# Half of the last matrix product's columns by seven products, with sums of blocks of m as the stationary operand

## The chip, the cores and the metric

One core of a Trainium2 chip runs the kernel. The metric is the device time of one execution in microseconds (us); lower is better. The engines that matter are TensorE (PE in the profile, with its weight loads as PEld), VectorE (DVE), ScalarE (ACT), GpSimd (POOL, which here issues transfers) and SyncE (SP, which issues the loads of the weights). SBUF is the on-chip memory, PSUM the accumulators that PE writes.

## The reference

One encoder layer for 512 positions of width 2048. The part that is changed is the last product; m comes from the two branches before it:

```python
m = jax.nn.sigmoid(ga) * ya + jax.nn.sigmoid(gb) * yb
x = x + jnp.einsum('bld,de->ble', m, w_o)      # m: 512 x 2048, w_o: 2048 x 2048
return rmsnorm(x, final_g)                      # over the 2048 columns of a row
```

Here `ya` is the output of a gated convolution through `w_out_a` (W_a), `yb` that of a state-space branch through `w_out_b`. All is float32.

## The kernel before

**Numbers in two parts.** Each float32 operand is split in a rounded part `hi` (ACT, a cast) and a rest `lo = x - hi` (DVE, a subtraction), and a product is the sum of three: hi x hi, hi x lo, lo x hi. An operand of the activations in two parts is called `pair` (128 x 2 x 512).

**Weights.** `WStream` holds the weights' loads in order. `W.get()` gives the two parts of the next block of 128 x 1024 numbers (512 KB); `_loads` issues the load on SP's queue (L527, tile `w_raw`), `_hi` the cast (L545, tile `w_hi`), `_lo` the subtraction (L562, `w_lo`). Parts are made two blocks ahead of their use (`ahead`), loads two blocks ahead of that (`lead`); `hi` and `lo` have four buffers each. `add7` gives a group of four blocks for seven products, and makes the sums of blocks that these need on DVE, in place.

**Seven products.** Most products, W_a's last twelve column blocks among them, already work so: a 2 x 2 arrangement of blocks is multiplied with seven block products instead of eight, with sums and differences of blocks as operands (`seven`, `product`, L931 and L936). There the weights are PE's stationary operand and the activations stream. Sums of the activations' blocks (tile `h_comb`) are made by `combine`, from a memory copy that is loaded in 256 KB pieces (tile `h_sum`).

**Order of the work.** The order is written out by hand: side work is a list `bg` of generators, and `step(n)` advances it by n steps between products. A scheduler then places each instruction in its engine's queue. The engines work through their queues in order.

**m and the output product.** `mix` makes m from W_a's product two column blocks at a time and stores it to memory (`m_d`). `reload_m` loads a 512 KB block of it (L1053, tile `m_r`, in the pool `r4b` of six buffers) and splits it into two `pair`s (`split`, L616 and L48). The first four blocks are reloaded during the last seven products of W_a; the last block is split without a trip to memory. Then `omm` multiplies: m is stationary (128 rows of it), 512 columns of W_o stream (L1102 to L1104). Three groups of 512 columns (`n4`) run with four accumulators, one per tile of 128 rows; the fourth group runs row tile by row tile, its weights kept in SBUF by a second stream `W2`, and the last row tile in two halves of 256 columns. `evac` adds x to the accumulator and sums squares; `add_up` and the lines behind it finish a row tile: root, scaling by row and by the gain `fg`, store.

**Buffers.** The large pool `r4` has 37 buffers of 4 KB per partition (`NR4`) for weights, pairs, sums, x and output. In the stage of W_a 16 hold `pair`s and 16 hold `h_comb`.

Of the kernel before, what the change touches and what calls it, by code (L numbers as in the profile page):

```python
# [461 lines left out]
class WStream:  # L462
# [20 lines left out]
    def add7(self, x11, x21, x22, x12):  # L483
# [29 lines left out]
        self.ops.append((lambda: b12["x"], b12, False, None))  # L513
        self.ops.append((lambda: b22["x"], b22, False, None))

    def _loads(self, upto):
        c, nc = self.c, self.c.nc
        while self.nl < len(self.loads) and self.loads[self.nl][0] <= upto:
            i, src, box = self.loads[self.nl]
            self.nl += 1  # L520
            n = src.shape[1] * src.shape[2] if len(src.shape) == 3 else src.shape[1]
            flat = src.rearrange("p a b -> p (a b)") if len(src.shape) == 3 else src
            raw = box["x"] = c.r4.tile([P, SLOT], F32, tag="r4", name="w_raw")
            first = self.ops[i][3]
# [54 lines left out]
def hybrid_kernel(ctx: ExitStack, tc: tile.TileContext, xT, x, cvec, fg, wu, wu7, wabc,  # L579
# [31 lines left out]
    def pair():  # L611
        t = c.r4.tile([P, 2, L], F32R, tag="r4", name="pair")
        return t
# [2 lines left out]
        act.copy(dst[:, 0], src)  # L616
        tt(dst[:, 1], src, dst[:, 0].bitcast(F32), SUB)

    W, W2 = WStream(c, 2, 2), WStream(c, 0, 0)
    for k in range(KD):  # L620
        W.add(wu[k], first=(lambda: scale_x(0)) if k == 0 else None)
    for h in range(2):
# [25 lines left out]
            W.add(wga[j, 2 + h])  # L648
    for j in range(NP7, KD, 2):
        W.add7(wga[j, 2], wga[j + 1, 2], wga[j + 1, 3], wga[j, 3])  # L650
    for n4 in range(4):
        for h in range(8):
            (W2 if n4 == 3 and h < 6 else W).add(wo[n4, h], resident=n4 == 3 and h < 6)


    cv_t = c.cst.tile([P, 106], F32, name="cvec_t")
# [389 lines left out]
        nc.gpsimd.dma_start(m_d[j // 2][:, j % 2], t)  # L1046
    while bg:
        step()
    mp = []

    def reload_m(i):
        t = wide("m_r")
        nc.gpsimd.dma_start(t, m_d[i])  # L1053
        yield
        for n in range(2):
            p = pair()
            split(p, t[:, n])
            mp.append(p)
            yield

    def mix(o, g, t, j):
        stt(g, g, 1.0, o, ADD, MUL)
        yield
        stt(t, t, 0.25, g, MUL, ADD)
        if j < KD - 2:
            nc.gpsimd.dma_start(m_d[j // 2], t)
        yield

    yb7 = blocks(yap, ty7)
    for j in range(NP7, KD, 2):  # L1070
# [6 lines left out]
    for i in range(4, 7):  # L1077
        bg.append(reload_m(i))
    while bg:
        step()  # L1080
    for n in range(2):
        p = pair()
        split(p, mq[-1][1][:, n])
        mp.append(p)


    fgt = [r4b.tile([P, 1024], F32, tag="r4", name="fg") for _ in range(2)]
    for i in range(2):
        nc.gpsimd.dma_start(fgt[i], fg[:, i * 1024:(i + 1) * 1024].to_broadcast([P, 1024]))
    ot = []  # L1090
    for t in range(4):
        for i in range(2):
            o = c.r4.tile([P, 1024], F32, tag="r4", name="o")
            nc.gpsimd.dma_start(o, x[t * P:(t + 1) * P, i * 1024:(i + 1) * 1024])
            ot.append(o)

    def omm(ps, t, w, kk, first, last, c0=0, c1=L):
        hi, lo = (v.rearrange("p (k n) -> p k n", n=L) for v in w)
        for k2 in range(2):
            a = mp[kk * 2 + k2]  # L1100
            cs = slice(t * P, (t + 1) * P)
            nc.tensor.matmul(ps, a[:, 0, cs], hi[:, k2, c0:c1], start=first and k2 == 0, stop=False)  # L1102
            nc.tensor.matmul(ps, a[:, 0, cs], lo[:, k2, c0:c1], start=False, stop=False)  # L1103
            nc.tensor.matmul(ps, a[:, 1, cs], hi[:, k2, c0:c1], start=False, stop=last and k2 == 1)  # L1104

    st = c.cst.tile([P, 4, 8], F32, name="st")

    def chunk(t, n4, a=0, b=L):
        return ot[t * 2 + n4 // 2][:, (n4 % 2) * L + a:(n4 % 2) * L + b]

    def gain(n4, a=0, b=L):
        return fgt[n4 // 2][:, (n4 % 2) * L + a:(n4 % 2) * L + b]

    def evac(ps, t, n4, i, a=0, b=L):
        o = chunk(t, n4, a, b)
        stt(o, ps, 0.25, o, MUL, ADD)
        sq = tmp()
        act.activation(sq[:, :b - a], o, AF.Square, accum_out=st[:, t, i:i + 1])

    def add_up(t, i, scale, bias):  # L1120

# [3 lines left out]
            tt(v, v, st[:, t, n:n + 1], ADD)  # L1125
        ts(v, v, scale, MUL, bias, ADD)

    for n4 in range(3):
        pss = [psum() for _ in range(4)]
        for kk in range(8):  # L1130
            w = W.get()
            for t in range(4):
                omm(pss[t], t, w, kk, kk == 0, kk == 7)
            if n4 == 1 and kk >= 4 or n4 == 2 and kk % 3 == 1:
                W2.prep()
        for t in range(4):
            evac(pss[t], t, n4, n4)
    wl = []
    for t in range(4):
        parts = [(0, L)] if t < 3 else [(0, L // 2), (L // 2, L)]  # L1140
        for n, (a, b) in enumerate(parts):
            ps = psum()[:, :b - a]
            for kk in range(8):
                if t == 0:
                    wl.append(W2.get() if kk < 6 else W.get())
                omm(ps, t, wl[kk], kk, kk == 0, kk == 7, a, b)
            if n == len(parts) - 1:

                add_up(t, 3 + n, 1.0 / D, EPS)
                for i in range(3):  # L1150
                    tt(chunk(t, i), chunk(t, i), gain(i), MUL)
                if a:
                    tt(chunk(t, 3, 0, a), chunk(t, 3, 0, a), gain(3, 0, a), MUL)
            evac(ps, t, 3, 3 + n, a, b)
        last = st[:, t, 2 + len(parts):3 + len(parts)]
        v, r, s = (st[:, t, i:i + 1] for i in (5, 6, 7))
        stt(v, last, 1.0 / D, v, MUL, ADD)
# [91 lines left out]
```

## Time and profile before

| | |
|---|---|
| runs | 1693.05, 1693.30, 1693.66 us, median 1693.3 |
| profiled execution | 1694.92 us in all, span 1693.1 us |
| PE, DVE, ACT busy | 1675.1, 1286.4, 722.4 us |
| matmuls | 8612 |
| moved by transfers | 233.53 MB, mean 138 GB/s |
| loads of W_o | 32 of 512 KB |

The span is the time from the first to the last instruction in the profile. "Busy" is the sum of an engine's instructions; instructions of one engine can overlap a little, so the starts of two that follow each other give the pace. "L931" is line 931 of the kernel. A row of the timeline has start, duration, engine, line, operation, output and inputs; in brackets stands how long the engine stood idle before and what ended that. The granted clock of PE is 1.00 at full rate.

### The profile page before, as it was taken

To read this page: it belongs to the slowest core of one execution; us is meant where nothing else is said; L and a number is where in the kernel's file an instruction comes from. 1 tells how busy PE (TensorE), PEld (TensorE's weight loads), DVE (VectorE), ACT (ScalarE), POOL (GpSimd) and SP (SyncE) were. 2 spreads that over 40 slices of the span, in tenths; PEclk is the share of its full clock that TensorE was granted. 3 is DMA by queue.
4 is the path that set the end of the run, shared out by engine and by line. 5 is a ranking of instruction groups with operands and counts; after the bars stand their busy time and mean duration, and the time that the engine had idled before them with its cause. 6 is when DMAs were issued, how large, how long until landed. Compare 5 with 4: busy or idle time off the path is not lost.

```text
span 1693.1 us, 22360 instructions
## 1 busy us (share of the span) xinstructions
PE 1675.1 (99%) x8612; PEld 1434.0 (85%) x8612; DVE 1286.4 (76%) x1889; ACT 722.4 (43%) x941; POOL 138.9 (8%) x240
## 2 busy tenths in 40 slices
PE   9999999999999999999999999999999999999997
PEld 7888888888888888888888888888888888878887
DVE  7895483948769777698989899998989699974333
ACT  6433423334316422454545554445545444453321
POOL 0003203040100021000000000000000220020000
PEclk9999999999999999999999999999999999999999
DMA  8324345353531454233333433333343855576212
GB/s 303 112 89 133 102 147 113 136 145 103 171 112 54 153 172 157 90 118 116 100 112 102 136 128 108 112 99 115 121 132 130 300 196 179 185 266 256 75 38 100
DMA packets 68331, 233.53 MB, mean 138 GB/s; under 512 B 9152, under 2 KB 9280, under 8 KB 68224
## 3 DMA queue, kind: packets, MB, share of 16 engines
q1 hardware_dynamic: 49392, 170.94, 30.2%
q0 software_dynamic: 18112, 60.06, 11.2%
q8 instruction: 67, 1.10, 0.3%
q10 hardware_dynamic: 720, 1.10, 0.2%
q14 instruction: 40, 0.33, 0.1%
HBM read 203.10 MB, written 24.77 MB: 135 GB/s over the span
## 4 chain that ended last, share of the span: by engine, by line
PE 92%; DVE 4%; DMA 2%; issue 1%; ACT 0%; DVEq 0%; POOL 0%; SPq 0%; ACTq 0%; POOLq 0%
PE ps L931 25%; PE ps L936 13%; PE ps L702 12%; PE ps L701 12%; PE ps L700 12%; PE ps L1103 3%; PE ps L1104 3%; PE ps L1102 3%; PE ps L778 1%; PE ps L779 1%; PE ps L777 1%; DVE w_lo L562 1%; DMA w_raw<-in_wga_dram 1%; PE ps L339 1%; PE ps L434 1%
## 5 line engine op out<-in xcount | busy, mean ns | idle before, releaser
L545 ACT CAST w_hi<-w_raw 128x1024 fp32r<-128x1024 f32 (+2 forms) x347 | 361.7, 1043 | 592.9 <-PE ps L701 246.2
L562 DVE TENSOR_TENSOR w_lo<-w_raw,w_hi 128x1024 fp32r<-128x1024 f32 (+2 forms) x347 | 418.5, 1210 | 242.6 <-ACT w_hi L545 241.9
L700 PE MATMUL ps<-pair,w_hi 128*128 128x512 f32 x912 | 355.8, 390 | 0.0
L702 PE MATMUL ps<-pair,w_lo 128*128 128x512 f32 x912 | 354.4, 389 | 0.7 <-DVE w_lo L562 0.7
L701 PE MATMUL ps<-pair,w_hi 128*128 128x512 f32 x912 | 354.7, 389 | 0.0
L931 PE MATMUL ps<-h_comb,w_hi 128*128 128x512 f32 x1216 | 305.3, 393 | 4.7 <-ACT half L951 4.2
L931 PEld LDWEIGHTS ps<-h_comb,w_hi 128*128 128x128 f32 x1216 | 218.9, 189 | 44.5 <-ACT half L951 4.6
L931 PE MATMUL ps<-pair,w_hi 128*128 128x512 f32 x912 | 230.1, 394 | 0.0
L702 PEld LDWEIGHTS ps<-pair,w_lo 128*128 128x128 f32 x912 | 171.2, 188 | 36.4 <-DVE w_lo L562 1.1
L700 PEld LDWEIGHTS ps<-pair,w_hi 128*128 128x128 f32 x912 | 171.3, 188 | 35.1
L701 PEld LDWEIGHTS ps<-pair,w_hi 128*128 128x128 f32 x912 | 171.3, 188 | 35.1
L931 PEld LDWEIGHTS ps<-pair,w_hi 128*128 128x128 f32 x912 | 165.3, 190 | 29.9
L936 PEld LDWEIGHTS ps<-h_comb,w_lo 128*128 128x128 f32 x1216 | 165.9, 190 | 11.9
L936 PE MATMUL ps<-h_comb,w_lo 128*128 128x256 f32 x1216 | 169.6, 282 | 0.0
L545 ACT CAST w_hi<-w_sum 128x1024 fp32r<-128x1024 f32 x76 | 79.9, 1051 | 139.4 <-DVE w_sum L501 61.5
L936 PEld LDWEIGHTS ps<-pair,w_lo 128*128 128x128 f32 x912 | 125.2, 191 | 9.0
L936 PE MATMUL ps<-pair,w_lo 128*128 128x256 f32 x912 | 127.8, 283 | 0.0
L562 DVE TENSOR_TENSOR w_lo<-w_sum,w_hi 128x1024 fp32r<-128x1024 f32 x76 | 92.6, 1218 | 7.2 <-ACT w_hi L545 7.2
L48 DVE TENSOR_TENSOR half<-ps,half 128x512 f32<-128x512 f32 x114 | 78.0, 684 | 7.2 <-PE ps L936 7.2
L1102 PE MATMUL ps<-w_hi,pair 128*128 128x512 f32 (+1 forms) x212 | 81.6, 385 | 0.0
L1103 PE MATMUL ps<-w_lo,pair 128*128 128x512 f32 (+1 forms) x212 | 81.6, 385 | 0.0
L1104 PE MATMUL ps<-w_hi,pair 128*128 128x512 f32 (+1 forms) x212 | 81.6, 385 | 0.0
(197 smaller groups left out, 1784.5 us busy)
## 6 DMA issues: line engine op xcount, KB each, us to landing
w_raw<-in_wabc_dram SPq DMA_DIRECT2D x128, 512.0 KB, 4.2
w_raw<-in_wga_dram SPq DMA_DIRECT2D x64, 512.0 KB, 4.3
w_raw<-in_wgb_dram SPq DMA_DIRECT2D x48, 512.0 KB, 4.2
w_raw<-in_wo_dram SPq DMA_DIRECT2D x32, 512.0 KB, 7.3
w_raw<-in_wgz_dram SPq DMA_DIRECT2D x24, 512.0 KB, 3.6
w_raw<-in_wu_dram SPq DMA_DIRECT2D x15, 448.0 KB, 7.5
xt<-in_xT_dram SPq DMA_DIRECT2D x16, 256.0 KB, 6.5
ga<-tmp POOLq DMA_DIRECT2D x16, 256.0 KB, 2.4
```

The lines of the kernel that those rows point to most:

```text
L48: return v.tensor_tensor(out=o, in0=a, in1=b, op=op)
L339: nc.tensor.matmul(ps[:, i * NCH:(i + 1) * NCH], self.sl[ri][:, q].rearrange("p g s -> p (g s)"), self.u4[:, q, :], start=True, stop=True)
L545: nc.scalar.copy(hi[:, a:b], raw[:, a:b])
L562: nc.vector.tensor_tensor(out=lo[:, a:b], in0=raw[:, a:b], in1=hi.bitcast(F32)[:, a:b], op=SUB)
L700: nc.tensor.matmul(ps, hi[:, k], a[:, 0], start=first and k == 0, stop=False)
L701: nc.tensor.matmul(ps, hi[:, k], a[:, 1], start=False, stop=False)
L702: nc.tensor.matmul(ps, lo[:, k], a[:, 0], start=False, stop=last and k == 7)
L931: nc.tensor.matmul(ps if flat else both, hi[:, k], a, start=first and k == 0, stop=False, skip_group_check=True)
L936: nc.tensor.matmul(ps[:, HL:], lo[:, k], a[:, :HL] if flat else a[:, 0], start=False, stop=last and k == 7, skip_group_check=True)
L1102: nc.tensor.matmul(ps, a[:, 0, cs], hi[:, k2, c0:c1], start=first and k2 == 0, stop=False)
L1103: nc.tensor.matmul(ps, a[:, 0, cs], lo[:, k2, c0:c1], start=False, stop=False)
L1104: nc.tensor.matmul(ps, a[:, 1, cs], hi[:, k2, c0:c1], start=False, stop=last and k2 == 1)
```

## The change

- Columns 0 to 1023 of the output (`n4` 0 and 1) are computed as before, but with the blocks of the sum in the order `KORD` = 0, 4, 1, 5, 2, 6, 3, 7.
- Columns 1024 to 2047 are computed by seven products. The 2 x 2 blocks of m are its two halves of 256 rows by its two halves of 1024 columns; those of W_o are 1024 x 512 blocks. m's blocks or sums of them (`tm`, tile `m_sum`) stay stationary, 128 rows at a time; W_o's blocks or sums of them stream. One product is 4 weight blocks x 2 row tiles x 6 matmuls.
- `add7_wide` loads the weights for it: 4, 8, 4, 4, 8, 4 and 4 loads for the seven products, since the blocks are loaded again where a sum needs them; 16 sums on DVE.
- m is loaded by `load_y` in two 256 KB pieces and split by `split_m` two steps after the load; the first two steps' buffers come from `r4` (`raw4`). `split_m(0, 2)` runs during the last seven products of W_a (1.7 steps per product instead of 2.7), `split_m(2, 8)` and `sum_m` (which loads all of m again) during the first two column groups, five steps per weight block. The last block of m goes through memory like the others. `fetch_m` is called after `seven` instead of ahead of it.
- `W2` and its resident weights are gone. Accumulators of one product are carried on into the next: `evac` reads them between products. The output rows 256 to 511 are finished after the sixth product, rows 0 to 127 within the seventh, and rows 128 to 255 at the end, in two halves of 256 columns.

The core of the diff:

```diff
-    for n4 in range(4):
-        for h in range(8):
-            (W2 if n4 == 3 and h < 6 else W).add(wo[n4, h], resident=n4 == 3 and h < 6)
+    for n4 in range(2):
+        for h in KORD:
+            W.add(wo[n4, h])
+    W.add7_wide(*([wo[n, 4 * h + i] for i in range(4)] for n in (2, 3) for h in range(2)))
+    def add7_wide(self, x11, x12, x21, x22):
...
+        for x in x11:
+            op(None, keep, (0, x))
+        for s, a, b in zip(sums, x21, x22):
+            op(s, set_(1, 2, ADD), (s, a), (0, b))
+        for s, a in zip(sums, x11):
+            op(s, set_(0, 1, SUB), (0, a))
+        for s, a in zip(sums, x12):
+            op(s, set_(1, 0, SUB), (0, a))
+        for a, b in zip(x11, x21):
+            op(None, set_(1, 2, SUB), (0, a), (0, b))
+        for xs in (x12, x22):
+            for x in xs:
+                op(None, keep, (0, x))
-    def reload_m(i):
-        t = wide("m_r")
-        nc.gpsimd.dma_start(t, m_d[i])
-        yield
-        for n in range(2):
-            p = pair()
-            split(p, t[:, n])
-            mp.append(p)
-            yield
+    def load_y(k, y):
+        for i in range(2):
+            nc.gpsimd.dma_start(y[:, i], m_d[k // 2 + 4 * i][:, k % 2])
+        return y
+    def split_m(a, b, buf):
+        q = []
+        for k in range(a, b + 2):
+            if k < b:
+                q.append(load_y(k, buf("m_r")))
+                yield
+            if k >= a + 2:
+                k, y = k - 2, q.pop(0)
+                for i, l in enumerate((m11, m12)):
+                    if k % 2 == 0:
+                        l.append(two("m_half"))
+                    d, v = l[-1][:, k % 2], y[:, 0, i * HL:(i + 1) * HL]
+                    act.copy(d[:, 0], v)
+                    tt(d[:, 1], v, d[:, 0].bitcast(F32), SUB)
+                yield
+                p = pair()
+                split(p, y[:, 1])
+                m2.append(p)
+                yield
+    def sum_m():
...
+                tt(t[:, 0], y12, y11, SUB)
+                tt(t[:, 1], y22, t[:, 0], SUB)
+                tt(t[:, 2], y22, y12, SUB)
+                tt(t[:, 3], y21, t[:, 1], SUB)
...
+    fetch_m()
     for j in range(NP7, KD, 2):
-        fetch_m()
-        if j == KD - 2:
-            for i in range(4):
-                bg.append(reload_m(i))
-        o = seven("wa", yb7, 2.7 if j == KD - 2 else 1.0)
+        end = j == KD - 2
+        if end:
+            bg.append(split_m(0, 2, raw4))
+        o = seven("wa", yb7, 1.7 if end else 1.0)
+        if j < KD - 2:
+            fetch_m()
         bg.append(mix(o, *mq[j // 2], j))
...
+    bg.append(split_m(2, 8, wide))
+    step(5.0)
+    bg.append(sum_m())
...
+    def product_o(pss, acts, first, last):
+        for i in range(4):
+            w = W.get()
+            for t in range(2):
+                omm(pss[t], acts[t][2 * i:2 * i + 2], w, first and i == 0, last and i == 3)
+    pb = [psum() for _ in range(2)]
+    product_o(pb, ym11, True, False)
+    for t in range(2):
+        evac(pb[t], t, 2)
+    pd = [psum() for _ in range(2)]
+    product_o(pd, tms[0], True, False)
+    for t in range(2, 4):
+        os_[t] = load_o(t, 1, c.r4.tile([P, 1024], F32, tag="r4", name="o"))
...
+    product_o(pb, tms[1], False, False)
+    for t in range(2):
+        evac(pd[t], 2 + t, 3)
+        evac(pb[t], 2 + t, 2)
+    product_o(pd, ym22, False, True)
+    for t in range(2):
+        evac(pd[t], 2 + t, 2)
+        square(2 + t, 2, 2)
+    product_o(pb, tms[2], False, True)
+    for t in range(2):
+        early(2 + t, 0)
+        evac(pb[t], 2 + t, 3)
+        evac(pb[t], t, 3)
+    pa = [psum() for _ in range(2)]
+    product_o(pa, ym21, True, True)
+    for t in range(2):
+        finish(2 + t, 0)
+    for t in range(2):
+        evac(pa[t], t, 2)
+        square(t, 2, 2)
+    ws = [W.get() for _ in range(4)]
+    for t in range(2):
+        for a, b in [(0, L)] if t == 0 else [(0, HL), (HL, L)]:
+            ps = psum()[:, :b - a]
+            for i in range(4):
+                omm(ps, tms[3][t][2 * i:2 * i + 2], ws[i], i == 0, i == 3, a, b)
...
+        finish(t, a)
```

`early` multiplies a row tile's first three column groups by the gain ahead of its last evacuation; `finish` is the root, the scaling and the store, as before.

More of the change, by code (lines that the diff above doesn't have):

```diff
@@ L36 @@
 NP7 = 4
+OSTEP = 5.0
+KORD = (0, 4, 1, 5, 2, 6, 3, 7)
 HL = L // 2
@@ L514, in add7, with op, make, set_ @@
         self.ops.append((lambda: b22["x"], b22, False, None))
+    def add7_wide(self, x11, x12, x21, x22):
+        tt = self.c.nc.vector.tensor_tensor
+        sums = [{} for _ in x11]
+        def op(acc, fn, *srcs):
+            boxes = [b if isinstance(b, dict) else {} for b, _ in srcs]
+            for b, (_, src) in zip(boxes, srcs):
+                self._load(src, b)
+            box = acc if acc is not None else boxes[0]
+            def make():
+                fn(box, *boxes)
+                return box["x"]
+            self.ops.append((make, box, False, None))
+        def set_(i0, i1, o):
+            def f(s, *b):
+                v = (s,) + b
+                tt(out=s["x"], in0=v[i0]["x"], in1=v[i1]["x"], op=o)
+            return f
+        keep = lambda s, *b: None
+        for x in x11:
[11 more added lines that the diff above has]
+                op(None, keep, (0, x))
     def _loads(self, upto):
@@ L1064, in mix, with raw4 @@
         stt(t, t, 0.25, g, MUL, ADD)
[L1065 to L1075 removed]
+        nc.gpsimd.dma_start(m_d[j // 2], t)
+        yield
+    def raw4(name):
+        t = c.r4.tile([P, 2, L], F32, tag="r4", name=name)
+        return t
@@ L1076, in hybrid_kernel @@
+    yb7 = blocks(yap, ty7)
+    fetch_m()
+    for j in range(NP7, KD, 2):
+        end = j == KD - 2
+        if end:
+            bg.append(split_m(0, 2, raw4))
+        o = seven("wa", yb7, 1.7 if end else 1.0)
+        if j < KD - 2:
+            fetch_m()
         bg.append(mix(o, *mq[j // 2], j))
-    for i in range(4, 7):
-        bg.append(reload_m(i))
     while bg:
         step()
[L1081 to L1097, printed above, removed]
-        hi, lo = (v.rearrange("p (k n) -> p k n", n=L) for v in w)
[L1099 to L1104, printed above, removed]
+    def lhs(k, h, t):
+        if k < 8:
+            return (m11, m12)[t // 2][k // 2][:, k % 2, h, (t % 2) * P:(t % 2 + 1) * P]
+        return m2[k - 8][:, h, t * P:(t + 1) * P]
@@ L1126, in add_up, with early, finish @@
         ts(v, v, scale, MUL, bias, ADD)
[L1128 to L1155, printed above, removed]
+    def early(t, a):
+        add_up(t, 4 if a else 3, 1.0 / D, EPS)
+        for i in range(3):
+            tt(chunk(t, i), chunk(t, i), gain(i), MUL)
+        if a:
+            tt(chunk(t, 3, 0, a), chunk(t, 3, 0, a), gain(3, 0, a), MUL)
+    def finish(t, a):
+        n = 4 if a else 3
+        square(t, 3, n, a)
         v, r, s = (st[:, t, i:i + 1] for i in (5, 6, 7))
-        stt(v, last, 1.0 / D, v, MUL, ADD)
+        stt(v, st[:, t, n:n + 1], 1.0 / D, v, MUL, ADD)
         act.activation(s, v, AF.Sqrt)
@@ new lines, in hybrid_kernel, with half @@
+    for t in range(4):
+        evac(pss[t], t, 1)
+        square(t, 1, 1)
+    for t in range(2):
+        os_[t] = load_o(t, 1, r4b.tile([P, 1024], F32, tag="r4", name="o"))
+    def half(blocks, l, c0=0):
+        return [[[b[:, h, t * P:(t + 1) * P] for h in range(2)] for b in blocks] for t in range(2)]
+    ym11 = half([m11[k // 2][:, k % 2] for k in range(8)], 0)
+    ym21 = half([m2[k][:, :, :HL] for k in range(8)], 0)
+    ym22 = half([m2[k][:, :, HL:] for k in range(8)], 0)
+    tms = [half([tm[i][k // 2][:, k % 2] for k in range(8)], 0) for i in range(4)]
@@ new lines, in hybrid_kernel @@
+    for i in range(2):
+        f = c.r4.tile([P, 1024], F32, tag="r4", name="fg")
+        nc.gpsimd.dma_start(f, fg[:, i * 1024:(i + 1) * 1024].to_broadcast([P, 1024]))
+        fgt.append(f)
+    product_o(pb, tms[1], False, False)
[11 more added lines that the diff above has]
+        evac(pb[t], t, 3)
```

72 lines of the change are left out of this document (65 added, 7 removed).

## The prediction

> **What bounds the kernel now.** I read the page first, then the windows of the tail, then the timeline of each engine around the one hole they show, then the chain and the transfers. The page (busy us, share of the span):
>
> ```profile
> span 1693.1 us, 22360 instructions
> PE 1675.1 (99%) x8612; PEld 1434.0 (85%) x8612; DVE 1286.4 (76%) x1889; ACT 722.4 (43%) x941; POOL 138.9 (8%) x240
> ```
>
> TensorE (PE) is busy for 99% of the span, so time can come only from fewer matmul columns or from the few holes. Windows of the steady part of the stage before the output product, and of the output product (window, its length, busy us of PE, PEld, DVE, ACT, POOL, granted clock, DMA share, GB/s):
>
> ```profile
> 1440.00:1460.00 20.00, 20.00 (x118) 17.62 (x117) 18.25 (x19) 9.29 (x11) 1.60 (x3) 1.00 0.57 191
> 1510.00:1684.00 174.00, 174.00 (x814) 145.99 (x814) 70.46 (x108) 49.78 (x77) 6.12 (x12) 1.00 0.37 136
> ```
>
> In the output product PE has no hole at all (174.00 of 174.00) and the vector engine (DVE) is only 70.46 of 174 busy. In the product with W_a, which already works by seven products, DVE is at 18.25 of 20 and PE still has no hole. Between the two lies the only hole inside the kernel:
>
> ```profile
> 1490.00:1492.00 2.00, 2.00 (x14) 1.81 (x13) 0.98 (x1) 0.00 (x0) 1.06 (x2) 1.00 1.02 403
> 1492.00:1494.00 2.00, 0.41 (x2) 0.00 (x0) 0.00 (x0) 0.02 (x1) 0.00 (x0) 1.00 1.01 399
> 1494.00:1496.00 2.00, 0.00 (x0) 0.00 (x0) 1.29 (x2) 2.00 (x4) 0.00 (x0) 0.90 1.00 360
> 1496.00:1498.00 2.00, 1.40 (x3) 1.16 (x4) 1.23 (x1) 1.03 (x3) 0.53 (x1) 0.50 1.01 379
> 1498.00:1500.00 2.00, 2.00 (x6) 1.56 (x5) 0.69 (x2) 1.14 (x2) 0.00 (x0) 0.50 0.80 303
> 1500.00:1502.00 2.00, 2.00 (x8) 1.71 (x8) 0.60 (x1) 0.73 (x1) 0.53 (x1) 0.50 0.12 43
> 1502.00:1504.00 2.00, 2.00 (x12) 1.75 (x12) 1.19 (x2) 1.36 (x3) 0.00 (x0) 0.90 0.82 246
> ```
>
> PE falls to 0.41 and 0.00 of 2 us, and behind that the clock stands at 0.50 for some 6.8 us (0.90, three times 0.50, 0.90). The timelines of ScalarE (ACT) and PE, and one row of the chain, name the cause:
>
> ```profile
> 1488.14 1.05 ACT L545 CAST w_hi<-w_raw 128x1024 fp32r<-128x1024 f32 x1
> 1493.98 1.14 ACT L616 CAST pair<-m_r 128x512 fp32r<-128x512 f32 x2 [4.79 <-DMA m_r<-m]
> 1495.97 0.57 ACT L951 COPY half<-ps 128x512 f32<-128x512 f32 x1
> 1485.61 8.30 DMA m_r<-m
> 1482.94 2.00 PE L931 MATMUL ps<-pair,w_hi 128*128 128x512 f32 x8
> 1485.73 2.00 PE L931 MATMUL ps<-h_comb,w_hi 128*128 128x512 f32 x8
> 1496.60 1.22 PE L931 MATMUL ps<-h_comb,w_hi 128*128 128x512 f32 x2 [4.19 <-ACT half L951]
> 1507.04 0.40 PE L1103 MATMUL ps<-w_lo,pair 128*128 128x512 f32 x1
> 1510.05 0.40 PE L1104 MATMUL ps<-w_hi,pair 128*128 128x512 f32 x1
> ```
>
> ACT ends a weight cast at 1489.19 and stands before the split of m (L616) until 1493.98, because the load of m issued at 1485.61 took 8.30 us. Behind it in ACT's queue is the copy L951 that PE waits for: 4.19 us. The last seven begin at 1482.94 and one product takes 2.79 us (1482.94 to 1485.73), so seven should end at 1482.94 + 19.53 = 1502.47. They end at 1510.05 less the two output matmuls that were slipped in (0.46), 1509.59. The hole and its slow clock together cost **7.1 us**.
>
> **The change, part by part.**
>
> *Matmuls.* Pace of the output product, 24 and 51 matmuls apart:
>
> ```profile
> 1562.44 0.39 PE L1104 MATMUL ps<-w_hi,pair 128*128 128x512 f32 x1
> 1567.88 0.39 PE L1104 MATMUL ps<-w_hi,pair 128*128 128x512 f32 x1
> 1678.10 0.28 PE L1104 MATMUL ps<-w_hi,pair 128*128 128x256 f32 x1
> 1684.22 0.28 PE L1104 MATMUL ps<-w_hi,pair 128*128 128x256 f32 x1
> ```
>
> 5.44/24 = 0.2267 us for 512 columns, 6.12/51 = 0.120 us for 256. Before: 8 weight blocks x 4 row tiles x 6 matmuls for each of four column groups, 768 in all. After: 384 for the first two groups, and seven products of 4 blocks x 2 row tiles x 6 = 48, 336. That is 48 fewer, 48 x 0.2267 = 10.88. Before, the last row tile runs in halves of 256 columns: 96 x 0.120 - 48 x 0.2267 = 0.64 extra; after, only the last half product does: 0.32 extra. Together **-11.2 us**, all on PE's path. PE then needs 87.0 us for the first two groups and 6.5 x 10.88 + 5.76 = 76.5 us for the seven.
>
> *The hole.* m is now loaded as two 256 KB pieces, into buffers of the large pool instead of the six `r4b` ones, and its split is written two steps behind the load. The nearest row is the same shape of load, `h_sum` from `yag`:
>
> ```profile
> DMA to landing us min/median/max: 2.8/3.4/6.8
> ```
>
> The buffers come free when the first product of the last seven ends (1485.73), as before. With 2.8 to 3.4 us the data is there when ACT comes free and nothing is lost; with the 6.8 us maximum it lands at 1492.5, 1.4 us before the old 1493.9, and the hole is 4.19 - 1.4 = 2.8. The clock fell about 3 us after PE stopped (inside 1494 to 1496, PE out since 1492.4), so such a hole would not halve it. Ends: 0 and the old 7.1. I take the middle of 0 and 2.8, 1.4, since the transfers of `wo` compete here as before: **-5.7 us**.
>
> [...]
>
> *Splits and sums of m in the first two groups.* DVE gets 8 splits (two 256-column and one 512-column subtraction each) and 8 blocks of sums (four additions, four subtractions of 256). Rows:
>
> ```profile
> L48 DVE TENSOR_TENSOR h_t<-h_sum x32: 411/418/427, 590.9 to 1383.9; 128x256 f32<-128x256 f32 x32
> L869 POOL DMA_DIRECT2D h_sum<-yag x16: 537/537/544, 1344.6 to 1375.0; - x16
> 1488.64 1.22 DVE L56 SCALAR_TENSOR_TENSOR tb_r<-tb_r,ga_r 128x1024 f32<-128x1024 f32 x1
> 1489.77 1.21 DVE L562 TENSOR_TENSOR w_lo<-w_raw,w_hi 128x1024 fp32r<-128x1024 f32 x1
> 1553.42 0.68 DVE L56 SCALAR_TENSOR_TENSOR o<-ps,o 128x512 f32<-128x512 f32 x1
> 1554.02 0.68 DVE L48 TENSOR_TENSOR o<-o,fg 128x512 f32<-128x512 f32 x1
> ```
>
> 8 x (2 x 0.42 + 0.68) + 64 x 0.42 = 39 us, and 16 weight lows of 1.22 and 8 evacuations of 0.68 make 25: 64 of 87 us. It is hidden by PE's own 87 us; uncovered it would cost what exceeds them, none here. POOL issues 28 loads for the blocks that follow, 0.54 us each, nothing else waits in that queue but four loads of x. The block order 0, 4, 1, 5 gives PE 10.9 us per pair of blocks, more than a load (at most 8.30) and its split. **0**; bounds 0 and 3 (the first pair behind the prefetch of `wo`).
>
> *Seven products, DVE.* 28 weight lows and 16 sums of 128x1024, of which some 2 lows lie ahead: 42 instructions. Started back to back they are 1.13 us apart (1488.64 to 1489.77), the evacuations 0.60 (1553.42 to 1554.02). 42 x 1.135 = 47.7; 19 evacuations with those of the second group, 11.4; the gains of `early`, 4 x 3 x 0.60 + 0.33 = 7.5; small ones and three `finish` of about 2.0 each (2.8 from first to last in the rows below, with waits for ACT in it), 7.6; half a tile 0.7. Sum 74.9 of 76.5 us, 98%. From the second product to the fifth it is 4 x 2.27 = 9.1 for each 10.88, plus 1.2, 0, 2.4 and 1.2 for evacuations; the gains for the lower rows, 4.2, lie in the fifth and sixth. The backlog so grows to some 3.5 us. The four `lo` buffers let DVE be up to 8.2 us (three blocks of 2.72) early, less cast and low, 2.3: 5.9 us of cover. It nearly fits, but a wait for a late transfer comes out of the same cover. Rows for `finish`:
>
> ```profile
> 1663.63 0.16 DVE L56 SCALAR_TENSOR_TENSOR st<-st 128x1 f32<-128x1 f32 x1 [0.79 <-ACT tmp L1118]
> 1664.89 0.88 DVE L52 TENSOR_SCALAR o<-o,st 128x512 f32<-128x512 f32 x2
> 1665.69 0.74 DVE L56 SCALAR_TENSOR_TENSOR o<-o,st,fg 128x512 f32<-128x512 f32 x1
> ```
>
> I take **+3 us**; bounds 0 and 9 (rival 2).
>
> *Seven products, transfers.* 36 loads of 512 KB instead of 16, and x and the gains, 6 more. Rows of a full stretch:
>
> ```profile
> 1526.00:1528.00 2.00, 2.00 (x11) 1.65 (x10) 0.73 (x1) 1.05 (x1) 0.53 (x1) 1.00 1.03 422
> w_raw<-in_wo_dram SPq DMA_DIRECT2D x20, 512.0 KB, 12.6
> ```
>
> 24 loads belong to products two to five (8, 4, 4, 8), 12.6 MB, 6 others 3.1 MB: 15.7 MB in 43.5 us is 361 GB/s, under the 422 seen. Buffers of the large pool: 37, of which 32 hold m (4 + 4 + 8) and its sums (16), 5 are free. The four of `m12` come free at the end of the second group, those of `m11` one per block of the first product, then those of each used sum. So loads for products three to five can start ten and more us early. Its cover is this prefetch: **0**.
>
> *Accumulators.* Products alternate between two pairs, so that an evacuation of one pair runs beside a product on the other; nothing on PE. *Tail.* Last matmul 1684.22, span 1693.1: 8.9 us of evacuation, root, scaling and store, the same chain after. DVE has `finish` of row tile 0 (2.0 busy), `early` of tile 1 (2.4) and two evacuations in PE's last 5.76: **+0.5**, bounds 0 and 2. The moved `fetch_m` issues the same loads at the same place of POOL's queue: 0.
>
> Sum against the profiled execution: -11.2 - 5.7 + 3 + 0.5 = -13.4 on the span of 1693.1. That execution took 1694.92 in all; the median of the runs is 1693.3, 1.6 below, and I put the difference on the median: **1680**.
>
> **The rivals.**
>
> 1. *The hole stays.* ACT comes to the split before the load is there, as now. For: the same four `wo` loads start at the same moment (8.30 us against 3.4 for the like load). Against: smaller pieces, two blocks ahead. Time: 1693.3 - 11.2 + 3.5 = 1685.6.
>
> 2. *DVE bounds the seven products.* If the durations count and not the starts: 42 x 1.22 + 19 x 0.68 + 12 x 0.68 + 3 x 2.5 + 4 = 84 us against 76.5, +7.5 in place of +3. For: 98% even by starts. Against: 18.25 of 20 without a hole. Time 1684.4; with DVE waits for x on top up to 1690. [...]
>
> 3. *Slower: loads starve the sums.* If only the five free buffers turn over, with 12.6 us from issue to landing, 5 x 0.524 MB / 12.6 us = 208 GB/s; 24 loads then take 60.5 us instead of 43.5, +17.0. That alone uses up the gain (16.9), so below five turning buffers the kernel is slower; each hole long enough to halve the clock adds 7.1 - 4.2 = 2.9, two of them give 1693.3 - 16.9 + 17.0 + 5.8 = 1699. For: the sums hold four buffers from the second product to the fourth. Against: twelve more come free by then, and 12.6 us is the time in a saturated stretch, where the like load alone had 3.4.
>
> 4. *No change by rate:* 512-column matmuls with another stationary operand at the same 0.2267; nothing speaks for a slower pace.
>
> **How the numbers follow.** Forecast 0.56 (own range 1674.5 to 1683: the hole gone and no new wait gives 1693.3 - 11.2 - 7.1 = 1675.0), hole stays 0.18, DVE 0.14, starved 0.10, other 0.02. The range 1674.5 to 1690 takes in the first three. About 0.2% (3.4 us) is what a measurement of this kernel can tell from no change: faster than 1689.9 has the first two and most of the third, 0.84; slower than 1696.7 most of the starved case, 0.09; the rest 0.07.
>
> **What would show it.** Matmuls 48 fewer, 720 for the output; no PE hole near 1492 and clock 1.00 there, or a short one; ACT's wait at the split under 3 us. In the seven products PE full, DVE over 9 of 10; rival 2 shows PE waiting for a `w_lo` with DVE full, rival 3 PE waiting for `w_lo` with DVE idle behind `w_raw`, and SP waiting for a buffer. Wrong if the clock falls to 0.50 in the last 160 us.

## The result, and the profile after

The changed kernel takes 1679.35 us (median of 6 runs, 1675.43 to 1682.62) against 1693.17 (6 runs, 1690.57 to 1695.55): a ratio of 0.992, 95% interval 0.9904 to 0.9937. The forecast was 1680.0. The profiled execution took 1679.14 us, its span is 1677.4, 15.7 us shorter than the 1693.1 of before. From its page (busy us, share of the span, instructions):

```profile
span 1677.4 us, 22486 instructions
PE 1662.0 (99%) x8540; PEld 1422.3 (85%) x8540; DVE 1343.7 (80%) x1997; ACT 746.7 (45%) x993; POOL 152.8 (9%) x266
```

PE has 72 instructions fewer and 13.1 us less work; DVE has 57.3 us more. The windows of the changed kernel (window, length, busy us of PE, PEld, DVE, ACT, POOL, granted clock, DMA share, GB/s), first the whole output product, then the first, second and last of the seven products, then all seven:

```profile
1505.30:1668.90 163.60, 163.60 (x745) 136.31 (x744) 128.22 (x216) 74.99 (x131) 19.67 (x37) 1.00 0.67 233
1592.30:1603.20 10.90, 10.90 (x50) 9.03 (x49) 8.79 (x12) 5.58 (x10) 3.16 (x6) 1.00 0.70 225
1603.20:1614.10 10.90, 10.90 (x50) 9.03 (x49) 7.06 (x9) 4.22 (x4) 0.00 (x0) 1.00 0.99 371
1657.60:1668.90 11.30, 11.30 (x73) 10.19 (x71) 8.96 (x23) 4.55 (x11) 0.00 (x0) 1.00 0.52 157
1592.30:1668.90 76.60, 76.60 (x361) 64.28 (x359) 68.06 (x104) 36.41 (x54) 3.16 (x6) 1.00 0.62 222
```

PE is full in every row, at clock 1.00. The product takes 163.6 us where the prediction's paces give 87.0 + 76.5 = 163.5, and DVE is busy 68.06 of 76.60 in the seven products, 89%. The hole ahead of it is still there, only shorter. Windows of 2 us, then ACT's timeline (start, us; in brackets the idle time before it and what ended it), PE's, and one row of the chain:

```profile
1490.00:1492.00 2.00, 0.00 (x0) 0.00 (x0) 0.26 (x1) 0.70 (x2) 0.22 (x1) 1.00 0.96 281
1492.00:1494.00 2.00, 1.76 (x6) 1.44 (x7) 1.64 (x3) 1.11 (x3) 0.00 (x0) 0.77 0.95 358
1494.00:1496.00 2.00, 2.00 (x9) 1.71 (x8) 1.12 (x2) 1.16 (x3) 0.00 (x0) 0.50 1.03 418
1496.00:1498.00 2.00, 2.00 (x10) 1.69 (x10) 1.76 (x3) 2.00 (x5) 0.00 (x0) 0.88 1.02 416
```

```profile
1491.30 0.41 ACT L1115 CAST m_half<-m_r 128x256 fp32r<-128x256 f32 x1 [3.99 <-DMA m_r<-m]
1491.61 0.58 ACT L990 COPY half<-ps 128x512 f32<-128x512 f32 x1
1481.43 2.00 PE L972 MATMUL ps<-pair,w_hi 128*128 128x512 f32 x8
1492.24 3.09 PE L972 MATMUL ps<-pair,w_hi 128*128 128x512 f32 x8 [2.28 <-ACT half L990]
1505.23 0.40 PE L1182 MATMUL ps<-w_hi,m_half 128*128 128x512 f32 x1
1668.65 0.28 PE L1182 MATMUL ps<-w_hi,m_sum 128*128 128x256 f32 x1
1484.51 6.77 DMA m_r<-m
```

It is the same chain of causes as before: ACT stands 3.99 us before the first split of m, whose 256 KB took 6.77 us to land, and the copy that PE needs is behind the split. PE stands still 2.28 us, not 4.19, and the clock is at 0.50 for one stretch of 3.41 us instead of two. The last seven begin at 1481.43, should end 19.53 us later at 1500.96, and the output product starts behind them at 1505.23: 4.3 us lost, of which 2.28 + 3.41/2 = 4.0 is the hole and the clock; 0.3 is not assigned.

So the 15.7 us come from: output product -11.2 (174.9 us from 1509.59 to the end of the last matmul at 1684.50 before, 163.7 from 1505.23 to 1668.93 now); hole -2.8 (7.1 before, 4.3 now); tail -0.1 (8.5 us behind the end of the last matmul, 8.6 before); and, upstream of anything the change touches, -1.5 by which the last seven start earlier than before. These lie at the start of the kernel. Windows there, first of before, then of the changed kernel:

```profile
10.00:20.00 10.00, 7.48 (x26) 5.62 (x25) 8.07 (x10) 7.40 (x11) 0.00 (x0) 0.83 1.04 403
```

```profile
10.00:20.00 10.00, 7.94 (x35) 6.13 (x34) 8.67 (x11) 9.00 (x14) 0.00 (x0) 1.00 1.04 400
```

Before ran 3.4 us at half clock there in the profiled execution, the changed kernel none: a difference between two executions, not an effect of the change.

### The profile page after: what moved, and what is told of

It is laid out like the page before. It is cut to its first block, busy times and chain, and to the rows that moved or that the text cites. A ratio compares the mean times of both kernels' runs of the same rounds, so it can differ in the third digit from the quotient of the medians.

```text
span 1677.4 us, 22486 instructions
## 1 busy us (share of the span) xinstructions
PE 1662.0 (99%) x8540; PEld 1422.3 (85%) x8540; DVE 1343.7 (80%) x1997; ACT 746.7 (45%) x993; POOL 152.8 (9%) x266
## 4 chain that ended last, share of the span: by engine, by line
PE 96%; DVE 1%; DMA 1%; ACT 0%; issue 0%; DVEq 0%; SPq 0%; ACTq 0%
PE ps L972 28%; PE ps L977 15%; PE ps L743 12%; PE ps L741 12%; PE ps L742 12%; PE ps L1182 9%; PE ps L818 1%; PE ps L819 1%; PE ps L820 1%; PE ps L436 1%; PE ps L341 1%; PE ps L350 1%; PE ps L433 0%; DVE w_lo L602 0%; DMA w_raw<-in_wu_dram 0%; DMA m_r<-m 0%
## 5 line engine op out<-in xcount | busy, mean ns | idle before, releaser
L585 ACT CAST w_hi<-w_raw 128x1024 fp32r<-128x1024 f32 (+2 forms) x365 | 380.4, 1043 | 579.4 <-PE ps L742 245.1
L602 DVE TENSOR_TENSOR w_lo<-w_raw,w_hi 128x1024 fp32r<-128x1024 f32 (+2 forms) x365 | 440.3, 1210 | 186.9 <-ACT w_hi L585 186.4
L1182 PE MATMUL ps<-w_hi,pair 128*128 128x512 f32 x192 | 60.8, 389 | 0.0
L494 DVE TENSOR_TENSOR w_sum<-w_raw 128x1024 f32<-128x1024 f32 x38 | 46.5, 1225 | 14.9 <-DMA w_raw<-in_wga_dram 8.5
L1028 POOL DMA_DIRECT2D yag<-bg x8 | 4.3, 534 | 549.2 <-DVE bg L50 549.2
```

Of the source, the lines that this page charges most:

```text
L494: tt(out=bs["x"], in0=b21["x"], in1=b22["x"], op=ADD)
L585: nc.scalar.copy(hi[:, a:b], raw[:, a:b])
L602: nc.vector.tensor_tensor(out=lo[:, a:b], in0=raw[:, a:b], in1=hi.bitcast(F32)[:, a:b], op=SUB)
L1182: nc.tensor.matmul(ps, l, r[:, k2, c0:c1], start=first and k2 == i == 0, stop=last and k2 == 1 and i == 2, skip_group_check=True)
```

## The experiments

**Splits behind the copies.** Theory: the hole is ACT's queue order, the split standing before the copy. The changed kernel, with the first splits of m queued behind the last of those copies:

```
-        act.copy(e1[:, 1], pb)
+        late[:] = [act.copy(e1[:, 1], pb).ins]
...
+            if k == b and a == 0:
+                yield
...
-                    act.copy(d[:, 0], v)
+                    with tc.issue_after(late[0]):
+                        act.copy(d[:, 0], v)
...
-                split(p, y[:, 1])
+                with tc.issue_after(late[0]):
+                    split(p, y[:, 1])
```

> Only the place of the first splits of m in ScalarE's queue changes: they are queued behind the copy of the third product's accumulator (the last copy that PE needs early). Theory 1 (the rest of the hole is ScalarE standing before a split whose load has not landed, with a copy that PE needs behind it): no PE hole near 1490, granted clock 1.00 throughout the stage, and about 4.3 us less than the changed kernel, near 1675. Rival (the data of m is late in itself, the hole moves to the start of the output product): the same 1679, with PE waiting there.

1677.23 us (1676.37 to 1679.09), ratio 0.9908 (0.9893 to 0.9923). The hole is gone, clock 1.00. Its waits of PE (total, times, longest) and DVE's timeline name what is late next:

```profile
1490.00:1505.00 15.00, 15.00 (x84) 13.02 (x83) 13.05 (x18) 8.20 (x15) 3.21 (x6) 1.00 1.02 396
PE ps L1188 <- DVE w_lo L602: 1.7, 1, 1.7
1602.64 0.69 DVE L58 SCALAR_TENSOR_TENSOR o<-ps,o 128x512 f32<-128x512 f32 x1 [2.32 <-DMA o<-in_x_dram]
1609.22 0.69 DVE L50 TENSOR_TENSOR o<-o,fg 128x512 f32<-128x512 f32 x1 [3.62 <-DMA fg<-in_fg_dram]
```

PE is full between 1490 and 1505, so the queue order was the cause. Of the 4.3 us some half arrives (2.1 by the medians; the intervals overlap): DVE now stands behind the loads of x and of the gains in the second of the seven products, and a weight low behind them is 1.7 us late for PE.

**No lag.** The same mechanism from the other side: the first two blocks of m are split right behind their load, as before the change.

```
-        for k in range(a, b + 2):
+        lag = 2 if a else 0
+        for k in range(a, b + lag):
...
-            if k >= a + 2:
-                k, y = k - 2, q.pop(0)
+            if k >= a + lag:
+                k, y = k - lag, q.pop(0)
```

> The first two blocks of m are split right after their load instead of two steps later; all else as changed. Theory 1 (the scheduler decides the place in the queue by its own idea of when a load lands, and the hole is set by when the load lands): 1679 to 1680, the hole 2.3 to 2.7 us. Rival (the two steps of distance are what shortened the hole): the hole is back at 4.2 us with 6.8 us of half clock, 1682 or more.

1682.11 us (1680.6 to 1685.23), ratio 0.9939 (0.9926 to 0.9951).

```profile
PE ps L972 <- DVE half L50: 5.1, 1, 5.1
PE ps L972 <- ACT half L990: 0.7, 1, 0.7
1490.54 0.71 ACT L1116 CAST m_half<-m_r 128x256 fp32r<-128x256 f32 x2 [2.13 <-DMA m_r<-m]
1501.20 0.71 ACT L1116 CAST m_half<-m_r 128x256 fp32r<-128x256 f32 x2 [5.55 <-DMA m_r<-m]
1501.64 0.76 DVE L50 TENSOR_TENSOR m_half<-m_r,m_half 128x256 fp32r<-128x256 f32 x2 [5.56 <-ACT m_half L1116]
```

PE waits 5.8 us in all, 3.5 more than in the changed kernel, but at another place. Before the first split ACT stands 2.13 us instead of 3.99, and PE only 0.7. The second block's split then stands 5.55 us: DVE's part of it waits for ACT's, and behind that in DVE's queue is the evacuation that PE needs. So the two steps of lag make the waiting shorter as a whole, not the wait before the first split; what the smaller loads did is not shown apart from it. By the runs the lag is worth some 2.8 us, with overlapping intervals.

**The copies first, in the kernel before.** If the queue order is all, before should gain its 7.1 us by it alone.

```
-            split(p, t[:, n])
+            with tc.issue_after(late[0]), tc.issue_after(late[1]):
+                split(p, t[:, n])
```

(`late` holds the two copies, L949 and L951 in the kernel before; the edit also puts five steps between the first load of m and the next ones.)

> The kernel before, with one edit: the first splits of the reloaded m are queued on ScalarE behind the two copies of the accumulators that PE needs. Theory 1 (the hole before was ScalarE standing in front of a split, nothing else): the hole of 4.2 us and its slow clock go, 7.1 us less than before, 1686; the seven products alone are then worth 1686 less the 1677.2 of the first experiment, 8.9 us or, with the 1.7 us that PE waited there for w_lo, 10.6 of the 11.2 that the matmul count gives. Rival (the transfers are full there, the wait moves to a later consumer of m): 1690 or more.

1692.98 us (1691.43 to 1695.08, 11 runs), ratio 0.9998 (0.9989 to 1.0007): no gain. Its waits of PE, PE's windows, POOL's timeline and ACT's:

```profile
PE ps L1109 <- DVE w_lo L562: 1.9, 1, 1.9
1490.00:1505.00 15.00, 15.00 (x87) 13.14 (x86) 5.79 (x7) 5.23 (x8) 1.59 (x3) 1.00 0.73 265
1507.56:1510.97 3.41, 1.51 (x7) 0.95 (x6) 3.41 (x6) 1.72 (x2) 0.15 (x2) 1.00 0.83 317
1510.97:1514.38 3.41, 3.41 (x9) 2.66 (x9) 2.94 (x5) 1.62 (x3) 0.97 (x3) 0.50 0.81 270
1499.32 1.05 POOL L1055 DMA_DIRECT2D m_r<-m  x2 [8.78 <-DMA m<-tb_r]
1504.79 1.14 ACT L616 CAST pair<-m_r 128x512 fp32r<-128x512 f32 x2 [7.81 <-DMA m_r<-m]
1507.29 1.99 ACT L545 CAST w_hi<-w_raw 128x1024 fp32r<-128x1024 f32 x2
```

The hole at 1492 is gone and another stands at 1508: the next two loads of m are issued at 1499.32, behind a write of m (8.78 us of waiting on POOL), ACT stands 7.81 us before their split, and now a weight cast is behind the split in place of a copy. Before issued its second load at 1490.67, so the five steps may have a part in the new hole, and the run is not a test of the order alone. The trace's price is 1.9 + 3.41/2 = 3.6 us, half of the old 7.1, and the profiled span is 3.5 shorter (1689.6), but that execution also had clock 1.00 at the start; over 11 runs nothing is left of it. Why the runs show none of the remaining gain stays open, but the mean granted clock on record narrows it: 0.995 in the profiled execution of before, from which the 7.1 us were read, and 0.997 in the median both of these 11 runs and of the 15 of before beside them. So a usual run of before has less slow clock than that trace (0.002 of 1693 is 3.4 us, with what stands behind the last matmul counted in), and 7.1 us may be too high a price for its hole. The run does show that this edit gave the kernel before nothing that a measurement can tell. That the changed kernel's gain comes from the matmuls is read from the output product itself, 174.9 us before and 163.7 after, with PE full in both.

**DVE's room.** The prediction priced DVE's 98% at +3. Sixteen additions of 128x1024 that nothing uses (18.2 us at the 1.14 us of back-to-back starts) are put behind sixteen sums of weights:

```
+                if left[0] > 0:
+                    left[0] -= 1
+                    w = v[-1]["x"]
+                    tt(out=w, in0=w, in1=w, op=ADD)
```

> Behind each of the 16 sums of weight blocks stands one more 128x1024 addition on VectorE, 16 x 1.135 = 18.2 us more VectorE work inside the seven products; its result is used by nothing. Theory A (VectorE is at 98% of the seven products, some 6 us of cover in its buffers): PE starts to wait for w_lo and loses 10 to 18 us, 1689 to 1697. Rival (VectorE had room, the prediction counted work there that really lies elsewhere): within 3 us of the changed kernel.

1686.32 us (1684.48 to 1686.86), ratio 0.9958 (0.9945 to 0.9972): 7.0 us more than the changed kernel, neither the 10 to 18 of a full DVE nor the 3 or less of a free one. Its waits of PE:

```profile
PE ps L1188 <- DVE o L58: 2.1, 1, 2.1
PE ps L1188 <- DVE w_lo L608: 1.9, 2, 1.6
PE ps L978 <- ACT half L996: 1.5, 1, 1.5
PE ps L978 <- ACT half L998: 1.4, 1, 1.4
```

Only the first two, 4.0 us, are DVE's; another 1.4 us stand at the end, where 9.9 us instead of 8.5 follow the last matmul. By the medians about 11 of the 18.2 us were absorbed, but not all within the seven products: they start at 1591.07, and three of the additions ran before that (1572.97, 1579.77 and 1584.16), where DVE has slack (busy 66.21 of the 90 us from 1510 to 1600). The changed kernel had room for the rest.

**Fewer buffers.** Rival 3 of the prediction has the loads starved. Four of the large buffers were to be held until the last product, by a write at the start and a read at the end:

```
+                hold = [raw4("hold") for _ in range(4)]
+                for h in hold:
+                    nc.gpsimd.memset(h[:, 0, :8], 0.0)
...
+    for h in hold:
+        act.copy(warm, h[:, 0, :1])
```

> Four buffers of the large pool are held from the third block of the second column group to the last product, so that one instead of five is left for weights until the accumulators of the second group are done. Theory B (loads have room, the twelve buffers that come free in time carry them): within 2 us of the changed kernel. Rival (the five free buffers carry the loads): the weights of the first and second product come late, PE waits, 17 us or more are lost, 1696 and up, with the clock at 0.50 in places.

1680.99 us (1676.96 to 1682.33), ratio 0.9925 (0.9911 to 0.9938): 1.6 above the changed kernel, with overlapping intervals. But the timelines of POOL and ACT show that the buffers were not held:

```profile
1555.45 0.11 POOL L1261 MEMSET hold<- 128x8 f32 x1 [7.43 <-DVE w_lo L602]
1555.83 0.10 POOL L1261 MEMSET hold<- 128x8 f32 x1 [0.28 <-ACT warm L1324]
1557.06 0.19 ACT L1324 COPY warm<-hold 128x1 f32<-128x1 f32 x1 [0.20 <-POOL hold L1261]
```

The reads that release the buffers (L1324) were placed right behind the writes: the second write waits for the first read, and the last read is over at 1557.25, ahead of the seven products. So this run does not test rival 3. What speaks against it is the changed kernel: it had just the five free buffers that the rival reckons with, and PE, which the rival has waiting for `w_lo`, is full in the whole output product.

**The gains held back.** In the kernel with the splits behind the copies, DVE waits for the gains (3.62 us) with weight lows behind. Here the multiplications of `early` are queued behind the evacuation after the fourth product:

```
-        stt(o, ps, 0.25, o, MUL, ADD)
+        return stt(o, ps, 0.25, o, MUL, ADD)
...
+        with tc.issue_after(held[0]):
+            for i in range(3):
+                tt(chunk(t, i), chunk(t, i), gain(i), MUL)
...
+        held[:] = [evac(pd[t], 2 + t, 2).ins]
```

> The first experiment's kernel, and the multiplications by the gain fg are queued on VectorE behind the evacuation after the fourth product, since the trace showed VectorE standing 3.6 us in the second product before a gain whose load had not landed. Theory 1 (VectorE's cover was used up by that wait and by one for x, not by its work): PE has no wait for w_lo, 1.7 us less than the first experiment, 1675.5. Rival (VectorE's work itself is at its limit, moving the gains into the busier fifth product makes it worse): 1677 to 1680, PE waiting near the fifth or sixth product.

1676.83 us (1675.86 to 1681.63), ratio 0.9908 (0.9894 to 0.9922): no gain that can be told. PE's waits, a window, and DVE's timeline:

```profile
PE ps L1188 <- DVE w_lo L602: 1.4, 1, 1.4
1610.00:1620.00 10.00, 8.59 (x39) 6.78 (x38) 6.88 (x8) 3.23 (x4) 0.00 (x0) 1.00 0.99 385
1614.45 1.23 DVE L538 TENSOR_TENSOR w_raw<-w_raw 128x1024 f32<-128x1024 f32 x1 [3.08 <-DMA w_raw<-in_wo_dram]
```

The wait for the gains was only in front of another: DMA is at 0.99 and the weights themselves come late (3.08 us). In the second product transfers are the limit, by 1.4 us.

**The same with sixteen additions more.** Both edits together, to size DVE's room without the gains' wait.

> The kernel with the gains held, and 16 more additions of 128x1024 on VectorE behind the sums of weight blocks, 18.2 us of work that nothing uses. In the changed kernel VectorE was busy 68.1 of the 76.6 us of the seven products, not 75. Theory A2 (room of 8.5 us and some 3 of cover): 18.2 less 8.5 to 11.5, so 7 to 10 us more than the kernel with the gains held, 1682 to 1686. Rival (no room, as the prediction counted): 14 us or more on top, 1690.

1683.04 us (1682.32 to 1685.65), ratio 0.9943 (0.9928 to 0.9958): 6.2 more than without the additions, a little under the 7 to 10 expected with room, far from 14. By the medians twelve of 18.2 us are absorbed; what the trace shows as lost is mainly one wait and its clock (a hole of 3.96 us, then 0.50 for 6.83 us).

**Plain order of blocks.** The prediction counted on the order 0, 4, 1, 5 as cover for the loads of m. The kernel with the splits behind the copies, with `KORD = (0, 1, 2, 3, 4, 5, 6, 7)`:

> The first experiment's kernel with the weight blocks of the first two column groups in plain order 0 to 7. The prediction put nothing on the splits of m because the order 0, 4, 1, 5 gives PE 10.9 us per pair of blocks of m. Theory C (that order is the cover): the second block of weights needs m's third and fourth block 5.4 us after the start, loads and splits need more, PE waits 3 to 8 us near 1510, 1680 to 1687. Rival (the splits come early enough anyway): within 1 us of the first experiment.

1678.11 us (1676.13 to 1678.3), ratio 0.9909 (0.9895 to 0.9922), the same. PE waits 1.7 us for a `m_half` (longest 1.5) and the time is lost in the spread: the order is worth no more than that.

**What a hole costs.** The prediction's weakest step was the price of a hole. Here, in the kernel with the splits behind the copies, ScalarE copies old accumulators into the new ones ahead of three of the seven products, 3, 5 and 7 times, and PE waits for it:

```
+    def gap(dst, src):
+        for i in range(3):
+            act.copy(dst[i % 2], src)
...
+    gap(pb, pss[3])
...
+    gap(pd, pb[1])
...
+    gap(pa, pb[1])
```

> ScalarE copies old accumulators into the new ones 3 times before the first, the second and the sixth of the seven products, so that TensorE stands still there; the copies change nothing that is used. At some 0.5 us a copy the three holes are about 1.4 us each, up to 1 us more where ScalarE is in the middle of a cast. Both theories: the clock stays 1.00, the time is that of the kernel with the splits behind the copies (1677.2) plus 3 x 1.4 = some 1681.5.

> The same with 5 copies, holes of about 2.4 us. Theory A of the prediction (the clock falls only behind a hole of some 3 us or more): clock 1.00 throughout, 1677.2 + 3 x 2.4 = 1684.4. Theory B (from the 2.28-us hole of the changed kernel: a hole over some 2 us already halves the clock for one stretch of 3.4 us, 1.7 us lost): 1684.4 + 3 x 1.7 = 1689.5. Theory C (it depends on where the hole lies in a fixed raster of 3.413 us): some of the three holes halve it and others of the same length do not, between the two.

> The same with 7 copies, holes of about 3.4 us. Theory A: each hole halves the clock for one stretch of 3.4 us, 1677.2 + 3 x (3.4 + 1.7) = 1692.5. Theory B: the same or two stretches, to 1697.6. Theory C: at least one stretch behind each hole, since a hole as long as the raster covers most of one step of it.

One execution each: 1689.46, 1698.73 and 1699.98 us. The holes came out longer than planned, since ACT did casts and squares before the copies: 4.28, 2.10, 3.33; 4.06, 3.08, 4.30; 6.93, 4.05, 5.28 us. So the expected times don't apply, but the clock can be read hole by hole. Windows of 0.25 us around each show where the clock stood at 0.50; every such stretch is 3.41 or 6.83 us long:

| kernel | hole from, us | clock 0.50 from, us |
|---|---|---|
| 3 copies | 1589.02, 4.28 | 1593.71, 3.41 |
| 3 copies | 1606.10, 2.10 | none |
| 3 copies | 1652.02, 3.33 | 1655.15, 3.41 |
| 5 copies | 1591.43, 4.06 | 1594.30, 6.83 |
| 5 copies | 1609.30, 3.08 | 1611.37, 6.83 |
| 5 copies | 1658.90, 4.30 | 1662.57, 6.83 |
| 7 copies | 1589.59, 6.93 | 1594.69, 6.83 |
| 7 copies | 1610.08, 4.05 | 1615.17, 3.41 |
| 7 copies | 1659.81, 5.28 | 1662.96, 6.83 |

The length of a hole does not decide: 4.28 us cost one stretch, 3.08 us two. Nor does it decide whether the clock falls at all: it fell behind the holes of 1.90 us (the kernel before with the copies first) and 2.28 us (the changed kernel), and not behind 2.10 us here and 2.14 us (the changed kernel with sixteen additions more, the wait for `o`). Within one run they start on a fixed raster: with 3 copies 61.44 us apart (1593.71 to 1655.15), with 5 copies 17.07 and 51.20, with 7 copies 20.48 and 47.79, which are 18.0, 5.0, 15.0, 6.0 and 14.0 times 3.413 us (61.44/18). Windows cut along it, for 3, 5 and 7 copies in turn:

```profile
1603.95:1607.36 3.41, 2.15 (x10) 1.45 (x8) 3.17 (x5) 1.75 (x3) 0.26 (x1) 1.00 0.91 258
1607.36:1610.78 3.42, 2.58 (x11) 2.16 (x12) 3.42 (x4) 1.27 (x3) 0.00 (x0) 1.00 0.97 370
```

```profile
1607.96:1611.37 3.41, 1.34 (x6) 0.76 (x5) 3.41 (x5) 2.03 (x4) 0.00 (x0) 1.00 0.92 276
1611.37:1614.78 3.41, 2.40 (x6) 1.93 (x7) 3.41 (x5) 1.44 (x3) 0.00 (x0) 0.50 0.99 399
1614.78:1618.19 3.41, 3.41 (x10) 2.65 (x9) 1.77 (x3) 0.29 (x1) 0.00 (x0) 0.50 0.62 229
```

```profile
1608.34:1611.76 3.42, 1.73 (x8) 1.11 (x6) 3.28 (x4) 1.75 (x4) 0.00 (x0) 1.00 0.94 283
1611.76:1615.17 3.41, 1.04 (x3) 0.67 (x4) 3.41 (x5) 2.81 (x6) 0.00 (x0) 1.00 0.99 372
1615.17:1618.58 3.41, 3.41 (x9) 2.64 (x8) 3.41 (x7) 0.00 (x0) 0.00 (x0) 0.50 0.73 275
```

The hole of 2.10 us is shared by two steps of the raster, PE busy 2.15 and 2.58 of 3.4 in them, and nothing follows. The hole of 3.08 leaves 1.34 of 3.41 in the first step, 39%: the next step is halved. In that one PE is busy 2.40 at half speed, which counts as 35%, and it stays halved one step more. The hole of 4.05 falls so that its first step still has 1.73 of 3.42, 51%, and keeps the clock; the second has 30%, the third is halved, full of work, and ends it. So theory C holds in these runs, and the steps cut from the traces agree on one rule, an estimate from them: a step is halved when PE's work in the step before it (busy time, by half where the clock is half) was under about 0.45. The closest cases are, from full speed, 44% (halved: 1507.56 to 1510.97 of the kernel before with the copies first) against the 51% above (kept) and, for the return to full speed, 41% (stays halved, with 5 copies) against 46% (returns, without the lag):

```profile
1662.57:1665.98 3.41, 2.78 (x6) 2.11 (x7) 0.80 (x8) 2.64 (x6) 0.00 (x0) 0.50 0.00 0
```

```profile
1505.37:1508.78 3.41, 3.13 (x7) 2.48 (x8) 3.41 (x5) 0.00 (x0) 0.00 (x0) 0.50 0.80 296
```

## Why the prediction was right

By its own terms, on the spans of the two profiled executions:

| term | predicted | measured |
|---|---|---|
| matmuls | -11.2 | -11.2 |
| hole and clock | -5.7 | -2.8 |
| splits and sums of m, transfers, first two groups | 0 | 0 |
| DVE in the seven products | +3 | 0 |
| tail | +0.5 | -0.1 |
| start of the kernel | none | -1.5 |
| sum | -13.4 | -15.6 (spans: -15.7) |

*The matmuls* carry it and were right to the tenth: pace and counts by width hold, as 163.6 us in the window of the output product shows. (The text's "720" counts by width; in instructions it is 744 instead of 816, 72 fewer.)

*The hole* is the step that was mis-sized, by 2.9 us. Its place and cause were right: the split in ACT's queue ahead of the copy, behind a slow load. Its length was also within its two ends: the load took 6.77 us, the maximum of the row it was priced from, and the hole was 2.28 us, where 0 to 2.8 was allowed and 1.4 taken. What failed is "such a hole would not halve it", the clock. That read the fall of the clock as a delay of about 3 us behind PE's stop. In the traces it falls at the end of a step of the raster: in the changed kernel the step from 1489.65 to 1493.07 held the whole hole, PE busy 1.14 of 3.42 us, 33%, and the next was halved.

```profile
1489.65:1493.07 3.42, 1.14 (x7) 0.81 (x6) 1.33 (x2) 1.20 (x3) 0.54 (x1) 1.00 0.95 301
1493.07:1496.48 3.41, 3.41 (x13) 2.92 (x12) 1.93 (x5) 2.25 (x4) 0.00 (x0) 0.50 1.03 418
```

Rival 1, the hole stays, was therefore 4.3 parts of 7.1 true. The load of m was also little quickened by smaller pieces: half the bytes took 6.77 us instead of 8.30, beside `wo` with DMA at 0.95.

*DVE* was mis-sized the other way, by 3 us. The 74.9 us counted in the seven products came to 68.06. Most of the difference is instructions that ran ahead, in the end of the second group: only 12 of the 16 sums and 25 of the 28 weight lows stand between 1592.30 and 1668.90. That makes 37 where 42 were counted, 5 x 1.135 = 5.7 us less. PE never waited for DVE in the output product, and rival 2 falls with it. The sixteen extra additions show the room: by the medians 11 to 12 of 18.2 us vanish, some of it ahead of the seven products.

*Transfers* at 0 were right for the time but near their edge: in the second product DMA is at 0.99 and DVE stands 3.11 us for the gains, which only its cover hides.

```profile
1610.37 0.69 DVE L50 TENSOR_TENSOR o<-o,fg 128x512 f32<-128x512 f32 x1 [3.11 <-DMA fg<-in_fg_dram]
```

As soon as the hole is taken away and the products start earlier, that cover is gone and PE waits 1.4 to 1.7 us there.

*The tail* was read 0.3 us too long: its 8.9 us run from the start of the last matmul, 8.6 from its end. Nothing changed there. The clock does fall to 0.50 within the last 160 us, which the prediction named as a sign of being wrong, but only behind the last matmul, as in the kernel before, where it costs PE nothing (0.50 from 1673.97 to the end at 1677.4, and from 1686.73 to 1693.1 before; the last matmul ends at 1668.93 and 1684.50). Two of its other signs failed: ACT's wait at the split was 3.99 us and not under 3, and DVE was busy 89% and not over 9 of 10.

That the forecast of 1680.0 is so close to 1679.35 is partly luck. The two mis-sized terms, 2.9 too hopeful and 3 too careful, cancel. On the spans the sum is still 2.3 us short (13.4 against 15.7), mostly by the 1.5 us of the start, which is no effect of the change. The medians meet because the profiled execution of before was 1.6 us above its median. The matmul term is not luck.

## What to carry to other kernels

Where PE is 99% busy, count matmul columns first: here that term came out to the tenth. A load that an engine waits for in order holds whatever is queued behind it (the copy, and with it PE for 4.19 us before and 2.28 in the changed kernel); moving the waiting instruction only helps if what it is moved in front of can wait as long, so look for who is behind it at the new place before pricing the gain (with the copies first, a weight cast and 1.9 us of PE). Look in the trace, too, whether an edit did what it was meant to do: the buffers above were released as soon as they were taken. Price a hole of PE with its clock: here, from the last seven products on, holes of up to 1.73 us and those of 2.10 and 2.14 us left it at 1.00, while those of 1.90, 2.28 and 3.08 us and more were followed by one or two steps of 3.41 us at 0.50, each of which costs 1.7 us (3.41/2, an estimate) where it is full of work.

## What the runs showed of the hardware

In the three runs with copies ahead of the products, the stretches at clock 0.50 start 5.0, 6.0, 14.0, 15.0 and 18.0 times 3.413 us apart within a run (61.44/18 us), and each is one or two such steps long (3.41 or 6.83 us). In the steps cut from the traces, PE's work was 0 to 44% where the next step stood at 0.50, and 46% or more where it stood at 1.00; the 0.45 between them is an estimate from these steps. PE need not stand still for a whole step: 44% busy was halved (1.51 of 3.41 us, the kernel before with the copies first). That hole of 1.90 us is estimated to cost 3.6 (1.9 + 3.41/2). The same work can also run at another clock in another execution: the start is the same in all these kernels, and between 10 and 20 us the mean clock is 0.83 (3.4 us at half clock) in the trace of before and in that of the gains held with sixteen additions more, but 1.00 in those of the changed kernel, of before with the copies first, of the gains held and of the plain order. What spreads the runs of the changed kernel over 7 us stays open, since only one execution of each kernel has a trace. Slow clock can be half of it at most, by an estimate from the clocks on record: the mean granted clock is 0.998 both in its fastest run (1675.43 us) and in its slowest (1682.62). The rounding of that figure leaves 1.7 us (0.001 of 1680) between them. The half clock behind the last matmul, which enters the mean and costs nothing, leaves another 1.5 (it counts for 1.7 us in the trace of the changed kernel and 3.2 in that of before).
